# Combining three attention branches in the layout of the widest dilation instead of the plain order

## The chip, the cores and the metric

The kernel runs on one core of one Trainium2 chip. The metric is the device time of one execution in microseconds; less is better. A core has five engines that run side by side, each with its own ordered list of instructions: TensorE (PE in the profile; PEld is its loading of weights), VectorE (DVE), ScalarE (ACT), GpSimd (POOL) and SyncE (SP). SP computes nothing here; it issues nearly all DMA transfers, in order, and waits in that order for what each transfer needs. "SPq" marks its rows.

## The reference, cut to what matters

One decoder layer: a gated short convolution beside an attention mixer, then an output projection and a SwiGLU feed-forward part. The change touches only the attention. Each of 8 heads evaluates three branches, a window of 128 keys at distances of 1, 4 and 16 positions, and the three results are combined per position:

```python
DILATED_BRANCHES = ((128, 1), (512, 4), (2048, 16))      # window, dilation
SEQ, N_HEADS, HEAD_DIM = 2048, 8, 64

def dilated_mixture(q, k, v):
    outs, lses = [], []
    for window, dil in DILATED_BRANCHES:
        o, lse = dilated_branch(q, k, v, window, dil)    # query t sees keys t, t-dil, ..., t-window
        outs.append(o)
        lses.append(lse)
    w = jax.nn.softmax(jnp.stack(lses, axis=0), axis=0)
    o = jnp.sum(w[..., None] * jnp.stack(outs, axis=0).astype(jnp.float32), axis=0)
    return o.astype(q.dtype)
```

## The kernel before

The work goes in stages: input projection and convolution (to about 280 us of the profiled span), attention (about 280 to 805 us), output projection, and the feed-forward part (from about 970 us to the end). A scheduler fixes the order of each engine's instructions when the kernel is built, from the order in which the code asks for them and its own estimate of durations; the chip then keeps to that order.

In the attention stage the heads go in pairs: `g` is 0 to 3, `h` is 0 or 1, so heads are numbered 0 to 7 here as 2g + h. `attn_steps(g)` is a generator that computes the three branches `b` of the two heads: b = 0 is dilation 1, b = 1 dilation 4, b = 2 dilation 16. While it runs, `attention_pairs` interleaves the projections of the next pair (`qkv_steps`; tiles `mm`, matmuls of 128x384 from lines 187 to 189), or, beside the last heads, the rest of the convolution and the first output projections. So PE has two kinds of work in the stage, and what attention can't feed at once the projection fills.

A branch has 16 blocks of 128 queries. For b = 1 and b = 0 most steps take two blocks with two key blocks each; b = 1 has 7 steps, b = 0 has 8, and b = 2, where a block sees one key block, has 4 steps of four blocks. A step is a chain over all engines: PE makes the scores (`s`, lines 604 and 605), DVE adds the mask and takes the row's minimum (line 610, `accum_out` into column 65 of `u`), ACT takes the exponential (line 615), ACT and DVE split it into two halves (`eh`, lines 625 and 626), a DMA transposes them (`et<-eh`, issued by SP from line 195), and PE multiplies by the values (`av`, line 633). Steps of four blocks transpose on PE instead (`pt`, line 620; DVE then writes `et` at line 622). ACT copies `av` into the branch's result tile `u` (line 636), which holds 128 partitions x 16 blocks x 66 columns (64 outputs, the denominator, the minimum) in 32 bits, 528 KB in all.

The blocks of a branch lie in the branch's own layout. In b = 0, block n and partition p hold position 128n + p. In b = 2, block n and partition p hold position 16p + n. Before, the results are combined in the layout of b = 0: the branches run in the order 1, 2, 0; the results of b = 1 and b = 2 are stored to DRAM (`d_u<-u`, lines 642 and 645) and read back in the layout of b = 0 (`r<-d_u`, line 647), and `combine` runs when b = 0 is done. In `combine` DVE takes the minimum of the three columns 65 (lines 540 and 541), then three differences (543), ACT an exponential, POOL weights and adds the results (548 to 550, 554), and SP stores 64 columns for this head to `d_y` (557). For the last head DVE does POOL's part, four blocks at a time, and the result stays on chip (`y7`).

The tiles `r1` and `r2` have one buffer each, `u` has three, `v` (the branch's values, loaded from `d_v` by lines 518, 521 and 525) two, `mm` three.

Of the kernel before, what the change touches and what calls it, by code (L numbers as in the profile page):

```python
# [8 lines left out]
F32 = mybir.dt.float32  # L9
# [8 lines left out]
P = 128  # L18
# [3 lines left out]
NT = S // P  # L22
# [3 lines left out]
HD = 64  # L26
# [3 lines left out]
class Builder:  # L30
# [55 lines left out]
    def vmax(self, *xs):  # L86
# [4 lines left out]
        for i, x in enumerate(xs):  # L91
            e.tensor_reduce(a[:, i:i + 1], x, axis=AX.X, op=ALU.max, apply_absolute_value=True)
        if len(xs) == 2:
# [4 lines left out]
        q = self.wsm.tile([P, 1], F32, name="vm_q")  # L98
        e.tensor_reduce(q, t, axis=AX.X, op=ALU.max)
        r = self.wsm.tile([P, 1], F32, name="vm_r")  # L100
# [167 lines left out]
    def conv_steps(self, j, W, before=None, scratch=None):  # L268
# [12 lines left out]
        for c in range(S // NC):  # L281
# [25 lines left out]
            else:  # L307
# [11 lines left out]
            nc.sync.dma_start(self.d_ya[:, j, t], y)  # L319
            nc.vector.tensor_reduce(self.yamax[:, j * 4 + c:j * 4 + c + 1], y, axis=AX.X, op=ALU.max,  # L320
                                    apply_absolute_value=True)
# [119 lines left out]
    def qkv_steps(self, g, st):  # L441
# [12 lines left out]
        for i in range(0, NT, 4):  # L454
# [21 lines left out]
            ss = self.at.tile([P, 16], F32, name="qk_ss")  # L476
            nc.vector.tensor_reduce(ss, n, axis=AX.X, op=ALU.add)
            nc.vector.tensor_scalar(ss, ss, 1.0 / HD, EPS, op0=ALU.mult, op1=ALU.add)
# [28 lines left out]
    def attn_steps(self, g, st):  # L507

        nc = self.nc
        uv = self.at.tile([P, 1], F32, name="uv")  # L510
        nc.vector.tensor_scalar_mul(uv, st["u"], 2.0 ** 20)
        V, U, R = {}, {}, {}

        def load_v(h, b):
# [7 lines left out]
            else:  # L522

                for r in range(4):
                    nc.sync.dma_start(t[32 * r:32 * r + 32], dv.rearrange("(n p r) c -> r p n c", n=NT, r=4)[r])
        for h, b in [(h, b) for h in range(2) for b in (1, 2, 0)]:
            qT = st["qT"][h]
            ka, kl = (st[x][:, :, h] for x in ("ka", "kl"))
            load_v(h, b)
# [2 lines left out]
            last = g == 3 and h == 1  # L532

            def combine(c, n):

                ts = slice(c, c + n)
                bm = self.at.tile([P, NT], F32, name="bm", bufs=2)[:, 0:n]
                w = self.at.tile([P, 3, NT], F32, name="cw", bufs=2)[:, :, 0:n]
                X = [r[:, ts] for r in (U[h, 0], R[h, 1], R[h, 2])]
                nc.vector.tensor_tensor(bm, X[0][:, :, HD + 1], X[1][:, :, HD + 1], op=ALU.min)  # L540
                nc.vector.tensor_tensor(bm, bm, X[2][:, :, HD + 1], op=ALU.min)
                for q in range(3):
                    nc.vector.tensor_tensor(w[:, q], bm, X[q][:, :, HD + 1], op=ALU.subtract)
                nc.scalar.activation(w, w, AF.Exp)
                X = [x[:, :, 0:HD + 1] for x in X]
                e = nc.vector if last else nc.gpsimd
                for q in range(3):
                    e.tensor_tensor(X[q], X[q], w[:, q].unsqueeze(2).broadcast_to([P, n, HD + 1]), op=ALU.mult)
                e.tensor_tensor(X[1], X[1], X[2], op=ALU.add)
                e.tensor_tensor(X[0], X[0], X[1], op=ALU.add)  # L550
                nc.vector.reciprocal(bm, X[0][:, :, HD])
                nc.vector.tensor_scalar_mul(bm, bm, uv)
                y = self.y7[:, ts] if last else X[0][:, :, 0:HD]
                e.tensor_tensor(y, X[0][:, :, 0:HD], bm.unsqueeze(2).broadcast_to([P, n, HD]), op=ALU.mult)
                if not last:
                    i = (2 * g + h) * HD
                    nc.sync.dma_start(self.d_y.rearrange("(t p) c -> p t c", p=P)[:, :, i:i + HD], y)
            Ub = U[h, b] = self.up.tile([P, NT, HD + 2], F32, name="u", bufs=3)
            Vb = V[h, b]

# [26 lines left out]
            for u0 in (0, 8, 4, 12) if last and b == 0 else range(0, NT, 4):  # L587
# [48 lines left out]
                nc.scalar.copy(Ub[:, u0:u0 + 4, 0:HD + 1], av)  # L636
                if last and b == 0:
                    combine(u0, 4)
            if b > 0:
                du = self.d_u[2 * g + h][b - 1]  # L640
                if b == 1:
                    nc.sync.dma_start(du.rearrange("(n p r) c -> p n (r c)", n=4, r=4),
                                      Ub.rearrange("p (n r) c -> p n (r c)", n=4))
                else:
                    nc.sync.dma_start(du.rearrange("(p r) c -> p (r c)", r=16), Ub.rearrange("p r c -> p (r c)"))
                t = R[h, b] = self.up.tile([P, NT, HD + 2], F32, name=f"r{b}")
                nc.sync.dma_start(t, du.rearrange("(b p) c -> p b c", p=P))
            elif not last:
                combine(0, NT)

# [547 lines left out]
```

## Time and profile before

| what | value |
|---|---|
| median of 3 runs | 2199.84 us (2195.81 to 2200.91) |
| the profiled execution's own time | 2202.29 us |
| its span in the profile | 2200.5 us |
| mean granted TensorE clock | 0.981 |
| PE busy | 2070.1 us (94%) |
| DVE / ACT / POOL busy | 1454.9 / 1027.3 / 629.6 us |
| DMA packets | 555492, of them 354624 under 512 B |

The profiled execution lies 2.45 us above the median, within what the three runs scatter. Times inside the profile count from the start of the span. A matmul's row gives its whole passage through the array, so rows of consecutive matmuls overlap; how often PE can start one is read from the distance of their starts.

### The profile page before, as it was taken

To read this page: it belongs to the slowest core of one execution; us is meant where nothing else is said; L and a number is where in the kernel's file an instruction comes from. 1 tells how busy PE (TensorE), PEld (TensorE's weight loads), DVE (VectorE), ACT (ScalarE), POOL (GpSimd) and SP (SyncE) were. 2 spreads that over 40 slices of the span, in tenths; PEclk is the share of its full clock that TensorE was granted. 3 is DMA by queue.
4 is the path that set the end of the run, shared out by engine and by line. 5 is a ranking of instruction groups with operands and counts; after the bars stand their busy time and mean duration, and the time that the engine had idled before them with its cause. 6 is when DMAs were issued, how large, how long until landed. Compare 5 with 4: busy or idle time off the path is not lost. (4 is left out here: it accounts for less than half of the span.)

```text
span 2200.5 us, 32856 instructions
## 1 busy us (share of the span) xinstructions
PE 2070.1 (94%) x11864; PEld 1076.9 (49%) x11864; DVE 1454.9 (66%) x3380; ACT 1027.3 (47%) x2134; POOL 629.6 (29%) x515
## 2 busy tenths in 40 slices
PE   4899999989989879989899999999999999999999
PEld 2344567767666534433344444444444444444444
DVE  5687447778876677874776676766676565555554
ACT  6443347677776656661443343334333344344341
POOL 0000133244343212230321122212222235555463
PEclk9999999999999989999899999999999999999999
DMA  9777358999989989789322332233223554251342
GB/s 244 168 211 241 104 125 149 190 178 192 185 157 223 205 191 299 231 245 254 105 96 91 104 113 88 95 102 107 90 95 104 192 188 151 60 190 53 116 143 96
DMA packets 555492, 339.64 MB, mean 154 GB/s; under 512 B 354624, under 2 KB 508224, under 8 KB 552896
## 3 DMA queue, kind: packets, MB, share of 16 engines
q1 hardware_dynamic: 550320, 337.45, 58.8%
q8 instruction: 93, 1.52, 0.3%
q10 hardware_dynamic: 5008, 0.08, 0.1%
q14 instruction: 71, 0.58, 0.1%
HBM read 161.24 MB, written 107.54 MB: 122 GB/s over the span
## 5 line engine op out<-in xcount | busy, mean ns | idle before, releaser
L1002 PEld LDWEIGHTS <-w 128*128 128x128 f16 x3696 | 363.3, 98 | 472.1 <-issue 27.5
L1002 PE MATMUL ps<-b,w 128*128 128x512 f16 x2112 | 466.8, 382 | 16.8 <-DMA b<-d_h 7.1
L1120 PE MATMUL ps<-b,w 128*128 128x512 f16 x1848 | 399.3, 379 | 0.9 <-DVE s L1138 0.8
L1002 PE MATMUL ps<-hb,w 128*128 128x512 f16 x1584 | 351.2, 382 | 10.4 <-DVE s L1008 9.3
L1120 PEld LDWEIGHTS <-w 128*128 128x128 f16 x1848 | 180.8, 98 | 219.2 <-issue 1.4
L895 POOL TENSOR_TENSOR t<-wq 128x512 f32<-128x512 f32 (+1 forms) x46 | 59.2, 1286 | 440.5 <-issue 207.7
L187 PE MATMUL mm<-wq,b 128*128 128x384 f16 x512 | 170.6, 333 | 6.7 <-DVE vs L471 6.7
L1008 DVE TENSOR_TENSOR s<-ps,s 128x512 f32<-128x512 f32 x220 | 150.1, 683 | 39.8 <-PE ps L1002 39.1
L188 PE MATMUL mm<-wq,b 128*128 128x384 f16 x512 | 170.4, 333 | 0.0
L189 PE MATMUL mm<-wq,b 128*128 128x384 f16 x512 | 170.3, 333 | 0.0
L1127 POOL TENSOR_TENSOR x<-x,s 128x512 f32<-128x512 f32 x72 | 103.9, 1444 | 185.0 <-DVE s L1138 130.5
L1128 DVE SCALAR_TENSOR_TENSOR x<-ps,a_u,x 128x512 f32<-128x512 f32 x96 | 71.9, 749 | 112.7 <-PE ps L1120 82.8
L615 ACT ACTIVATE s<-s,u 128x256 f32<-128x256 f32 (+1 forms) x224 | 97.9, 452 | 68.3 <-DVE u L610 47.4
L610 DVE CUSTOM_DVE_ANT_0 s<-s,mask,nkap 128x256 f32<-128x256 f32 (+1 forms) x224 | 104.3, 482 | 19.2 <-PE s L605 13.4
L187 PEld LDWEIGHTS <-b 128*128 128x128 f16 x768 | 84.2, 110 | 65.0 <-DMA b<-b 7.5
L188 PEld LDWEIGHTS <-b 128*128 128x128 f16 x768 | 84.3, 110 | 62.9 <-issue 13.9
L189 PEld LDWEIGHTS <-b 128*128 128x128 f16 x768 | 84.1, 109 | 56.8 <-issue 5.1
L633 PE MATMUL av<-v,et 128*128 128x65 f16 x1800 | 77.8, 195 | 31.3 <-DMA et<-eh 20.3
L187 PE MATMUL cvx<-b,wq 128*128 128x512 f16 (+1 forms) x200 | 76.9, 388 | 31.8 <-ACT kb L262 25.0
L912 ACT CAST w<-t 128x512 f16<-128x512 f32 x88 | 53.6, 615 | 108.6 <-PE ps L1002 86.9
L604 PE MATMUL s<-ka,qT 128*128 128x128 f16 (+1 forms) x408 | 91.3, 270 | 8.6 <-DVE eh L626 7.6
L1107 ACT CAST w<-t 128x512 f16<-128x512 f32 (+1 forms) x96 | 53.7, 580 | 92.2 <-PE ps L1120 75.1
(297 smaller groups left out, 3792.0 us busy)
## 6 DMA issues: line engine op xcount, KB each, us to landing
d_a<-a SPq DMA_DIRECT2D x88, 256.0 KB, 2.0
d_wd<-w SPq DMA_DIRECT2D x77, 256.0 KB, 2.1
wq<-d_a SPq DMA_DIRECT2D x64, 256.0 KB, 4.3
b<-d_wd SPq DMA_DIRECT2D x14, 1024.0 KB, 6.0
wraw<-in_w_in_dram SPq DMA_DIRECT2D x24, 512.0 KB, 6.8
d_h<-hl SPq DMA_DIRECT2D x24, 512.0 KB, 3.7
wq<-in_w_gate_dram SPq DMA_DIRECT2D x22, 512.0 KB, 5.3
wq<-in_w_up_dram SPq DMA_DIRECT2D x22, 512.0 KB, 5.4
```

Source lines behind the costliest of these rows:

```text
L187: self.pe = mm(ps, lhsT=lh(k), rhs=rh(k), start=k == ks[0], stop=False)
L188: mm(ps, lhsT=lh(k), rhs=rl(k), start=False, stop=False)
L189: mm(ps, lhsT=ll(k), rhs=rh(k), start=False, stop=k == ks[-1])
L604: nc.tensor.matmul(o, lhsT=query(u), rhs=hi[x], start=True, stop=False)
L610: nc.vector.tensor_tensor_reduce(sm[:, at[u]], sp[:, at[u]], mask[:, P - P * has_prev(u):256], accum_out=Ub[:, u, HD + 1:HD + 2], op0=ALU.add,
L615: nc.scalar.activation(sm[:, at[u]], sm[:, at[u]], AF.Exp, scale=-1.0, bias=Ub[:, u, HD + 1:HD + 2])
L633: self.pe_av = nc.tensor.matmul(av[:, u - u0], lhsT=p_, rhs=v_, start=n_ == 0, stop=n_ == len(ops) - 1)
L1002: nc.tensor.matmul(ps[self.BANK[n]], lhsT=w[:, x, k], rhs=b[:, y, k], start=first and k == 0 and q == 0, stop=k == 3 and q == 2, skip_grou ...
L1008: nc.vector.tensor_tensor(t, x, y, op=ALU.add)
L1120: nc.tensor.matmul(ps[self.BANK[n]], lhsT=L[n][:, x, f], rhs=B[n][:, f, y], start=first and f == 0 and q == 0, stop=f == n_f - 1 and q == ...
L1127: nc.gpsimd.tensor_tensor(o, o, s_, op=ALU.add)
L1128: nc.vector.scalar_tensor_tensor(o, bank, u, o, op0=ALU.mult, op1=ALU.add)
```

## The change

For all heads but the last (g = 3, h = 1) the branches run in the order 1, 0, 2, and the combination is made in the layout of b = 2. The result of b = 2 now stays in its tile `u`. The results of b = 1 and b = 0 pass through DRAM: b = 1 is stored as before, b = 0 is stored in 2048 pieces of 264 B, and both are read back with 16 consecutive rows, 4224 B, for each partition. The store of the head's output to `d_y` addresses rows in the new layout; it is as many pieces of 256 B as before. The last head is computed as before. Bytes are the same everywhere; numbers of instructions on the computing engines are too.

```diff
-        for h, b in [(h, b) for h in range(2) for b in (1, 2, 0)]:
+        for h, b in [(h, b) for h in range(2) for b in ((1, 2, 0) if g == 3 and h == 1 else (1, 0, 2))]:
...
-                X = [r[:, ts] for r in (U[h, 0], R[h, 1], R[h, 2])]
+                X = [r[:, ts] for r in ((U[h, 0], R[h, 1], R[h, 2]) if last else (U[h, 2], R[h, 1], R[h, 0]))]
...
-                    nc.sync.dma_start(self.d_y.rearrange("(t p) c -> p t c", p=P)[:, :, i:i + HD], y)
+                    nc.sync.dma_start(self.d_y.rearrange("(p r) c -> p r c", r=NT)[:, :, i:i + HD], y)
...
-            if b > 0:
-                du = self.d_u[2 * g + h][b - 1]
+            if b != (0 if last else 2):
+                du = self.d_u[2 * g + h][b == 1]
                 if b == 1:
                     nc.sync.dma_start(du.rearrange("(n p r) c -> p n (r c)", n=4, r=4),
                                       Ub.rearrange("p (n r) c -> p n (r c)", n=4))
+                elif b == 0:
+                    nc.sync.dma_start(du.rearrange("(t p) c -> p t c", p=P), Ub)
                 else:
                     nc.sync.dma_start(du.rearrange("(p r) c -> p (r c)", r=16), Ub.rearrange("p r c -> p (r c)"))
-                t = R[h, b] = self.up.tile([P, NT, HD + 2], F32, name=f"r{b}")
-                nc.sync.dma_start(t, du.rearrange("(b p) c -> p b c", p=P))
+                t = R[h, b] = self.up.tile([P, NT, HD + 2], F32, name=f"r{1 if b == 1 else 2}")
+                if last:
+                    nc.sync.dma_start(t, du.rearrange("(b p) c -> p b c", p=P))
+                else:
+                    nc.sync.dma_start(t.rearrange("p r c -> p (r c)"), du.rearrange("(p r) c -> p (r c)", r=16))
```

After the change the lines behind 526 have moved by one (610 is 611, 541 is 542, 633 is 634, 626 is 627), and those of the round trip by more: 645 is 648 for the last head and 646 for the new store of b = 0, 647 is 651 for the last head and 653 for the others.

The order of the instructions shifts over the whole attention stage. Two places. The first is DVE's list at the end of head 4, around the second minimum of `combine`, which waits for the second result to come back from DRAM (`r_6992` before, `r_7096` after; `vs` is the split of the next pair's values out of PE's `mm`, `qT` a copy of its queries).

```order
L610 ISA sm,u<-s,mask,nkap 128x128
L610 ISA u 128x1
L610 ISA s,u<-s,mask,nkap 128x256
L610 ISA u 128x1
L610 ISA s,u<-s,mask,nkap 128x256
L610 ISA u 128x1
L541 TENSOR_TENSOR bm<-bm,r_6992 128x16
L543 TENSOR_TENSOR cw<-bm,u 128x16
```

```order
L541 TENSOR_TENSOR bm<-u,r_6744 128x16
L611 ISA s,u<-s,mask,nkap 128x256
L611 ISA u 128x1
L623 TENSOR_TENSOR et<-pt,et 128x512
L502 COPY qT<-qp 128x512 x2
L471 SCALAR_TENSOR_TENSOR vs_2123<-mm,vs_2123 128x2x64 x2
L611 ISA s,u<-s,mask,nkap 128x256
L611 ISA u 128x1
L542 TENSOR_TENSOR bm<-bm,r_7096 128x16
```

Before, the minimum stood behind the four masks of head 5's first step and the two of its second; after, it stands behind the second step's two and one of the third's, with a write of `et`, two copies of `qT` and two splits of `vs` ahead of it, and the first step's four masks come behind it. The branch whose return it waits for was, before, followed on PE by the 8 steps of b = 0, and is now followed by the 4 steps of b = 2.

The second place is SP's list around the second round trip of head 0 (`d_u_1_66` and `r_3336` before, `d_u_0_65` and `r_3500` after).

```order
L195 DMA_TRANSPOSE et<-eh 128x8x128
L645 DMA d_u_1_66<-u 128x1056
L518 DMA v<-d_v_61 128x4x520
L647 DMA r_3336<-d_u_1_66 128x16x66
L195 DMA_TRANSPOSE et<-eh 128x8x128 x3
```

```order
L195 DMA_TRANSPOSE kb<-qkhl 128x8x128
L646 DMA d_u_0_65<-u 128x16x66
L653 DMA r_3500<-d_u_0_65 128x1056
L473 DMA d_v_62<-vs_2123 128x2x520
L525 DMA v<-d_v_61 32x16x130
L195 DMA_TRANSPOSE et<-eh 128x8x128 x3
```

Before, a transpose of b = 0 stood ahead of the store and three more behind the load; after, the round trip stands in the four steps of b = 2, which need no DMA transposes, its load directly behind its store, and the four loads of b = 0's values for the next head (line 525) begin behind it.

## The prediction

> **What bounds the kernel now.** I read the split of the span by stages first, since the page's 94% for PE is a mean over stages.
>
> ```profile
> 0.00:320.00 320.00, 277.47 (x1404) 147.84 (x1405) 205.51 (x517) 142.72 (x291) 37.62 (x57) 0.98 0.70 181
> 320.00:805.00 485.00, 436.72 (x4244) 318.60 (x4243) 361.67 (x1313) 319.61 (x848) 162.90 (x124) 0.96 0.94 186
> 805.00:1103.00 298.00, 268.96 (x1189) 118.52 (x1188) 208.68 (x394) 155.17 (x278) 62.78 (x49) 0.94 0.82 224
> 1103.00:2200.50 1097.50, 1086.92 (x5030) 491.94 (x5028) 679.08 (x1157) 409.77 (x721) 366.26 (x285) 1.00 0.35 114
> ```
>
> The columns are the stretch, its length, busy time of PE, PE's weight loads, DVE, ACT and POOL, then the granted clock, the share of the 16 DMA engines and GB/s. The change lies in the second row. There PE is busy 436.7 of 485.0 us, so at most 48.3 us of idle time, and what the clock loses, can be won. The chain of work that ended last begins at about 1103 us and doesn't reach this stage, so I go by what PE waited for in it, line by line, with total, times and longest in us:
>
> ```profile
> PE av L633 <- DMA et<-eh: 20.3, 19, 3.2
> PE s L604 <- DVE eh L626: 7.6, 5, 4.2
> PE mm L187 <- DVE vs L471: 6.5, 5, 1.9
> PE av L633 <- DMA v<-d_v: 4.9, 1, 4.9
> PE av L633 <- ACT u L636: 4.2, 3, 1.8
> ```
>
> These name the last link, not the cause. The cause of the worst of them shows in the order of time around the end of heads 3 and 4 (start, length, engine, line; in brackets the idle time ahead and what ended it):
>
> ```profile
> 554.18 0.19 DVE L541 TENSOR_TENSOR bm<-bm,r 128x16 f32<-128x16 f32 x1 [4.45 <-DMA r<-d_u]
> ...
> 551.83 0.84 PE L633 MATMUL av<-v,et 128*128 128x65 f16 x12 [2.23 <-DMA et<-eh]
> 554.62 0.48 PE L187 MATMUL mm<-wq,b 128*128 128x384 f16 x1 [1.95 <-DVE vs L471]
> 554.90 0.52 PE L188 MATMUL mm<-wq,b 128*128 128x384 f16 x1
> 555.22 0.52 PE L189 MATMUL mm<-wq,b 128*128 128x384 f16 x1
> ...
> 611.54 0.19 DVE L541 TENSOR_TENSOR bm<-bm,r 128x16 f32<-128x16 f32 x1 [3.45 <-DMA r<-d_u]
> ...
> 612.97 0.32 PE L187 MATMUL mm<-wq,b 128*128 128x384 f16 x1 [1.54 <-DVE vs L471]
> 620.53 0.37 PE L604 MATMUL s<-ka,qT 128*128 128x256 f16 x1 [4.23 <-DVE eh L626]
> ```
>
> DVE stands for 4.45 us at the second minimum of the combination, because the branch result has not come back from DRAM. Everything DVE does for PE is queued behind it: the splits `vs` that free `mm`, the halves `eh`. PE loses 2.23 + 1.95 us there and 1.54 + 4.23 us at the next head. It also comes back slow: at 554.90 and 555.22 the starts are 0.32 us apart, and the stretch's clock was half.
>
> ```profile
> 550.50:554.00 3.50, 0.84 (x12) 0.74 (x13) 0.00 (x0) 2.52 (x8) 0.00 (x0) 0.68 1.34 240
> 554.00:558.00 4.00, 3.38 (x11) 1.58 (x11) 3.45 (x9) 2.06 (x5) 2.79 (x2) 0.50 1.22 160
> ```
>
> So such a wait costs about 2 us more behind it (4 us at 0.50). In the whole stage DVE waited like this 15.1 us (the row stands below).
>
> **The change part by part.** *The round trip through DRAM.* Its links are the store of the second branch, the load of it, and for the new kernel the nearest rows: the output store, whose 2048 pieces of 256 B are like the new store's 2048 of 264 B, and the load of b = 2's values, which like the new load takes one long piece per partition (4160 B against 4224 B). First the old store (645), the old load (647), then the output store (557) and the values' load (521):
>
> ```profile
> L645 SPq DMA_DIRECT2D d_u<-u x8: 345/532/1397, 364.1 to 769.6; - x8
> DMA to landing us min/median/max: 3.1/4.5/5.3
> ...
> L647 SPq DMA_DIRECT2D r<-d_u x16: 364/422/3672, 352.1 to 774.4; - x16
>   DVE bm L541: 15.1, 8
> DMA to landing us min/median/max: 4.4/5.9/8.0
> ...
> L557 SPq DMA_DIRECT2D d_y<-u x7: 360/434/572, 394.6 to 751.9; - x7
> DMA to landing us min/median/max: 4.1/4.3/6.2
> ...
> L521 SPq DMA_DIRECT2D v<-d_v x8: 342/552/769, 319.7 to 739.6; - x8
> DMA to landing us min/median/max: 3.9/4.8/5.9
> ```
>
> Before: 4.5 + 5.9 us, and about 1.6 us by my estimate for ACT's copy of the last `av` and SP's queue, 12.0 us in all. After: 4.3 + 4.8 + 1.6 = 10.7 us. From both sides: 4.1 + 3.9 + 1.6 = 9.6 and 6.2 + 5.9 + 1.6 = 13.7 us.
>
> Against it stands the time that PE can go on. I counted along PE's rows in both orders from the last `av` of the branch that is sent away to the first PE row that needs something behind DVE's second minimum. The starts in this piece of the trace give the steps of the count:
>
> ```profile
> 544.84 0.33 PE L187 MATMUL mm<-wq,b 128*128 128x384 f16 x1
> 545.00 0.33 PE L188 MATMUL mm<-wq,b 128*128 128x384 f16 x1
> ...
> 545.97 0.27 PE L604 MATMUL s<-ka,qT 128*128 128x256 f16 x1
> 546.08 0.27 PE L605 MATMUL s<-kb,qT 128*128 128x256 f16 x1
> ...
> 546.41 0.98 PE L633 MATMUL av<-v,et 128*128 128x65 f16 x24
> 547.23 0.41 PE L620 MATMUL pt<-ident,sm 128*128 128x128 f32 x2
> 547.48 0.27 PE L604 MATMUL s<-ka,qT 128*128 128x256 f16 x1
> ...
> et<-eh SPq DMA_TRANSPOSE x110, 4.3
> ```
>
> That is 0.16 us for a 384-wide matmul, 0.11 for a 256-wide one, 0.82/24 = 0.034 for an `av`, 0.25/2 = 0.12 for a `pt`; where the need is an `eh`, 5.5 us go off for the transpose (4.3 in the last row, 1.2 by estimate for the split and SP's issue). The allowances for heads 0 to 6 come to 10.5, 7.7, 8.8, 10.4, 9.4, 14.1 and 13.4 us before, and 13.0, 7.4, 12.4, 11.3, 7.1, 15.0 and 8.2 us after. Their means are 10.6 and 10.6: four steps of b = 2 give no less room than eight of b = 0, since the scheduler put as much projection into them. With 12.0 us, PE is short by 1.5 + 4.3 + 3.2 + 1.6 + 2.6 = 13.2 us before; that is the size of the four waits quoted (9.95 us for heads 3 and 4) with some for the rest. With 10.7 us, it is short by 3.3 + 3.6 + 2.5 = 9.4 us after, in heads 1, 4 and 6. This term is 9.4 - 13.2 = -3.8 us. Its ends are 6.1 - 13.2 = -7.1 us at 9.6 us, and 0.7 + 6.3 + 1.3 + 2.4 + 6.6 + 5.5 - 13.2 = +9.6 us at 13.7 us.
>
> *The half clock behind waits.* Two waits of over 3 us before (heads 3 and 4) cost about 2 us each; after, heads 1 and 4 come out at 3.3 and 3.6 us. I take -0.5 us, between -4 (none left) and +4 us (four).
>
> *The packets.* Per head, a load of 2048 pieces becomes one of 128 twice, and a store of 128 one of 2048: 1920 fewer, 13,440 for seven heads.
>
> ```profile
> DMA packets 242383, 90.35 MB, mean 186 GB/s; under 512 B 220816, under 2 KB 238486, under 8 KB 242070
> ...
> q1 hardware_dynamic: 242326, 89.61, 93.1%
> ```
>
> At the stage's mean of 0.931 x 485 x 16 / 242,326 = 0.030 us per packet, that is at most 13,440 x 0.030 / 16 = 25 us less on each engine; by bytes, which stay, it is nothing. Long pieces take longer each, so I go for 10 us of 451, 2%. PE feels it only in its 20.3 us of waits for `et`: 2% to 5% of the transposes' 4.3 us, 0.1 to 0.2 us at 19 waits, up to -4 us. I take -1.0 us. The transfers also move: b = 0's values and the head's output now load the b = 1 steps, which need transposes, and b = 2's steps are relieved, which do not; so +2 us is the other end.
>
> *The end of the stage.* Behind the last `av` PE has, of the 96 matmuls of the first output projections, 31 left before and 39 after, while the last combination runs its chain to `y7` and on to the transposes. PE then waits for those:
>
> ```profile
> 812.38 0.61 PE L187 MATMUL mm<-b,b 128*128 128x512 f16 x1 [7.04 <-DMA b<-b]
> ```
>
> Eight more 512-wide matmuls at 0.16 x 512 / 384 = 0.22 us fill 1.7 of the 7.04 us, and the last `av` comes as much earlier. I take -1.7 us; 0 is the other end, if the last branch is late for its own reasons.
>
> *What costs nothing.* The output store has the same pieces; its landing hides behind the next head. POOL's share is the same, with 162.9 of 485 us busy. The first minimum (541 after) needs b = 1, back long before. SP waits for the store's landing ahead of the load, as before; queued behind it is now mostly traffic for later steps, no transposes of b = 2, so nothing on PE's path; if that cover is gone it costs up to the store's 4.3 us in a head. Order on PE from the middle of the output projections on is unchanged.
>
> **Sum.** -3.8 - 0.5 - 1.0 - 1.7 = -7.0 us. Against the profiled execution's own 2202.3 us that gives 2195.3; its offset to the median is 2.4 us, so for the median 2199.8 - 7.0 = 2192.8 us.
>
> **A rule that speaks against it.** The old store of b = 2 lands in 4.5 us and the output store with small pieces in 4.3 us, so small pieces cost no more here. The Trainium skill, "DMA: Bandwidth & Descriptors", section "Specifications", says that transfers under 512 B go below line rate because the DMA engine reads, modifies and writes; by that rule the new store would be the slower one. The rows disagree with it for this size of store, as far as landing shows it; what it would do is the first rival.
>
> **The rivals.** *Slower: the return of b = 0 comes late.* Between its last `av` and the end of the head stand 4 steps where there were 8. If the new store lands late, all allowances are missed. Price by round trip: at 13.7 us +9.6 us in the first term, +4 us of half clock, with the other two terms as they are +10.9, so 2210.7 us. It decides from about 12.5 us on, where the short times (0 + 5.1 + 0.1 + 1.2 + 5.4 + 4.3 = 16.1 us) eat what the other terms bring. For it: three allowances of 7 to 8 us. Against it: the landing rows above, and that store and load now follow each other directly. *No change: the waits only move.* PE's 20.3 us for `et` come back in b = 0, whose work now starts behind b = 1 with less projection between scores and `av` in heads 0 to 2, 14.5 us on the mean where it was 16.4 by the same count; with the first term at +0.8 us (12.0 us again, 14.0 us short), -0.5 us of half clock, and the gains of packets and tail lost in it, the time is about 2200.1 us. For it: DMA engines at 0.94, which leave no slack for a reordering.
>
> **How the numbers follow.** Forecast 0.46, no change 0.29, slower 0.25. This measurement can tell about 0.2%, 4.4 us, from no change. Of the forecast's case a little ends within that; I give faster 0.46, same 0.28, slower 0.26. The range reaches from -7.1 - 4 - 4 - 1.7 = -16.8 us, 2183 us, to the slower rival's 2210 us; the forecast's own range is 2185 to 2196 us.
>
> **What would show it.** Right: DVE's wait for `r` at the second minimum falls from 15.1 to about 10 us; the new store (646) lands in about 4.3 us, the new loads (653) in about 4.8; the wait at about 812 us falls to about 5.3 us; PE's idle time in the stage falls from 48 to about 42 us. Wrong: DVE waits over 4 us in heads 1, 4 and 6 with PE's `vs` and `eh` waits behind; or `et` waits of 20 us or more, now in b = 0.

## The result, and the profile after

The changed kernel takes 2238.74 us (median of four runs, 2237.22 to 2239.9), the kernel before 2200.38 us beside it: a ratio of 1.0177, 95% interval 1.016 to 1.0195, or 38 us slower. The forecast was 2192.8 us with 2183 to 2210 as range. It was wrong in sign, and the time lies outside the range.

The split by stages again, same columns as in the prediction. The last stage, 1097.5 us before, is cut off at its old length, so that the first row here (the kernel before) and the second (the changed kernel) cover the same work, from 320 us to the end of the output projection, to within a few us. The two rows behind them are of line 187 in the output projection, first before, then after (count, shortest, median and longest in ns, first and last start in us).

```profile
320.00:1103.00 783.00, 705.68 (x5431) 437.12 (x5431) 570.34 (x1707) 474.78 (x1125) 225.68 (x173) 0.96 0.89 201
```

```profile
320.00:1140.60 820.60, 713.78 (x5423) 440.86 (x5423) 560.35 (x1706) 477.80 (x1127) 224.15 (x173) 0.94 0.85 191
```

```profile
L187 PE MATMUL ps<-b,b x112: 379/379/634, 817.5 to 960.5; 128*128 128x512 f16 x112
```

```profile
L187 PE MATMUL ps<-b,b x112: 379/379/379, 855.5 to 997.9; 128*128 128x512 f16 x112
```

The stretch is 37.6 us longer, as the span is. These matmuls begin 38.0 us later and end 37.4 us later, so the loss is complete when the output projection begins; the projections of the first pair of heads begin at 239.9 us before and 241.1 after. All but about 1 us of the loss therefore lies in attention. Of the 37.6 us, PE's rows with work grew by 8.1 us (705.68 to 713.78, clock 0.96 to 0.94, with the same number of matmuls but for missing records). The rest is idle time: all of PE's waits in the stretch add up to 78.3 us before and 106.7 us after, +28.4 (the list of waits misses about 1 us of the rest).

What PE waited for in the changed kernel, total, times and longest in us:

```profile
PE s L605 <- DVE eh L627: 29.3, 14, 6.2
PE av L634 <- DMA et<-eh: 17.5, 16, 4.8
PE mm L187 <- DVE vs L471: 9.2, 5, 3.3
...
PE mm L187 <- ACT b L779: 5.0, 1, 5.0
```

The waits for transposes fell a little (20.3 before). The waits for the score buffers, which DVE's half `eh` frees, rose from 7.6 to 29.3. The new store (646), the new loads (653), and what DVE and SP waited for because of them:

```profile
L646 SPq DMA_DIRECT2D d_u<-u x7: 359/458/1368, 374.4 to 767.2; - x7
DMA to landing us min/median/max: 7.8/8.7/9.7
...
L653 SPq DMA_DIRECT2D r<-d_u x14: 332/342/720, 352.3 to 775.4; - x14
DMA to landing us min/median/max: 3.3/4.2/6.8
...
DVE bm L542 <- DMA r<-d_u: 21.2, 6, 7.8
...
SPq L653 <- DMA d_u<-u: 38.1, 8, 8.0
SPq L525 <- PE av L634: 24.0, 4, 7.2
```

The store lands in 8.7 us where I had put 4.3. SP stands 38.1 us for it (8.1 before), and 24.0 us at the value loads of b = 0 for the last `av` of b = 2 (4.6 us for an `av` before). The two rows of the kernel before:

```profile
SPq L647 <- DMA d_u<-u: 8.1, 6, 2.6
...
SPq L525 <- PE av L633: 4.6, 2, 4.1
```

One place shows what that does, the end of head 1, in order of time: SP, DVE, PE, and the clock of the wait and of the 2.8 us behind it.

```profile
443.22 0.38 SPq L518 DMA_DIRECT2D v<-d_v  x1
444.28 0.36 SPq L646 DMA_DIRECT2D d_u<-u  x1
452.75 0.33 SPq L653 DMA_DIRECT2D r<-d_u  x1
453.20 0.36 SPq L473 DMA_DIRECT2D d_v<-vs  x1
453.67 16.27 SPq L195 DMA_TRANSPOSE et<-eh  x4
...
457.16 0.19 DVE L542 TENSOR_TENSOR bm<-bm,r 128x16 f32<-128x16 f32 x1 [3.00 <-DMA r<-d_u]
...
462.23 0.37 PE L605 MATMUL s<-ka,qT 128*128 128x256 f16 x1 [6.16 <-DVE eh L627]
...
456.00:462.20 6.20, 0.07 (x3) 0.00 (x0) 4.90 (x19) 4.32 (x12) 2.58 (x2) 0.69 0.76 89
462.20:465.00 2.80, 1.89 (x8) 1.26 (x8) 2.80 (x5) 0.41 (x1) 1.23 (x1) 0.50 0.49 94
```

The store goes out at 444.28; the load behind it only at 452.75, and the four transposes of the next head's first steps behind both. DVE stands 3.00 us at the second minimum; masks, the combination's differences and the next pair's norms are queued behind it, and the `eh` that PE needs starts at about 461.5. PE stands 6.16 us and goes on at a clock of 0.50. It is the mechanism of the prediction's "slower" rival, at a larger size than that rival was given.

The chain of work that ended last says the same of the whole stage. In the kernel before it could be followed back to about 1103 us only; here it runs through attention, and through all seven of the new stores, 61.4 us in sum, with six of their loads behind them (start and length in us):

```profile
374.45 7.78 DMA d_u<-u
...
444.28 8.40 DMA d_u<-u
...
505.39 8.69 DMA d_u<-u
...
572.72 9.31 DMA d_u<-u
...
632.42 9.70 DMA d_u<-u
...
697.10 9.35 DMA d_u<-u
...
767.20 8.15 DMA d_u<-u
```

### The profile page after: what moved, and what is told of

It is laid out like the page before. It is cut to its first block, busy times and chain, and to the rows that moved or that the text cites. A ratio compares the mean times of both kernels' runs of the same rounds, so it can differ in the third digit from the quotient of the medians.

```text
span 2238.1 us, 32856 instructions
## 1 busy us (share of the span) xinstructions
PE 2079.5 (93%) x11864; PEld 1081.3 (48%) x11864; DVE 1446.4 (65%) x3380; ACT 1030.5 (46%) x2134; POOL 626.5 (28%) x515
## 2 busy tenths in 40 slices
DMA packets 542052, 339.64 MB, mean 152 GB/s; under 512 B 340288, under 2 KB 493888, under 8 KB 539456
## 4 chain that ended last, share of the span: by engine, by line
PE 56%; DMA 16%; DVE 13%; ACT 5%; issue 4%; SPq 4%; POOL 1%; DVEq 0%; ACTq 0%; POOLq 0%
PE ps L1008 25%; PE ps L1126 18%; DMA d_u<-u 3%; PE mm L187 3%; PE mm L188 3%; PE mm L189 2%; DMA et<-eh 2%; SPq L195 2%; DMA wq<-in_w_up_dram 2%; PE av L634 1%; DMA qp<-qkhl 1%; DMA wraw<-in_w_in_dram 1%; DMA r<-d_u 1%; DMA wq<-in_w_gate_dram 1%; DVE s L611 1%
## 5 line engine op out<-in xcount | busy, mean ns | idle before, releaser
L1008 PE MATMUL ps<-b,w 128*128 128x512 f16 x2112 | 466.5, 381 | 16.6 <-DMA b<-d_h 7.2
L605 PE MATMUL s<-ka,qT 128*128 128x128 f16 (+1 forms) x408 | 94.1, 275 | 30.2 <-DVE eh L627 29.3
L634 PE MATMUL av<-v,et 128*128 128x65 f16 x1800 | 80.2, 197 | 31.3 <-DMA et<-eh 17.5
L634 PEld LDWEIGHTS <-et 128*128 128x128 f16 x1800 | 73.5, 100 | 54.6 <-DMA et<-eh 22.2
```

The costliest lines, as they stand in the source:

```text
L605: nc.tensor.matmul(o, lhsT=query(u), rhs=hi[x], start=True, stop=False)
L634: self.pe_av = nc.tensor.matmul(av[:, u - u0], lhsT=p_, rhs=v_, start=n_ == 0, stop=n_ == len(ops) - 1)
L1008: nc.tensor.matmul(ps[self.BANK[n]], lhsT=w[:, x, k], rhs=b[:, y, k], start=first and k == 0 and q == 0, stop=k == 3 and q == 2, skip_grou ...
```

## The experiments

"Leaves out" in a text on record tells which part of the computation a kernel doesn't do. The letters of theories are those of these texts. They speak of lines of 64 B: that size is an assumption of mine, which the sizes tried fit; no run measures it.

**1. What a store of small pieces costs by itself.** A kernel of nothing but transfers, one at a time, five times round, 128 partitions x 16 pieces:

```diff
+nc.sync.dma_start(a264.rearrange(tp, p=P), u)                                # 264 B, packed
+nc.sync.dma_start(b264.rearrange(tp, p=P)[:, :, 0:64], u[:, :, 0:64])        # 256 B at 264 B steps
+nc.sync.dma_start(c256.rearrange(tp, p=P), u[:, :, 0:64])                    # 256 B, packed
...
+nc.sync.dma_start(e320.rearrange(tp, p=P)[:, :, 0:66], u)                    # 264 B at 320 B steps
+nc.sync.dma_start(f320.rearrange(tp, p=P), w)                                # 320 B, packed
...
+nc.sync.dma_start(h264.rearrange("(p r) c -> p (r c)", r=NT), u.rearrange("p r c -> p (r c)"))
```

> This kernel does none of the layer: it only stores and reloads a tile through DRAM, one transfer at a time, five times each, so that each landing time stands alone. Stores: (33) 264 B pieces packed at 264 B, as the changed kernel stores b = 0; (35) 256 B pieces at steps of 264 B; (37) 256 B pieces packed; (39) 256 B pieces at steps of 2048 B, as the output store; (41) 264 B pieces at steps of 320 B; (43) 320 B pieces packed; (45) 264 B pieces at steps of 512 B; (47) 4224 B for each partition, as before; (49) 512 B pieces packed. Theory A, pieces that begin or end inside a 64 B line are what is slow: 33 and 35 about 7 us, 41 and 45 about 6 to 7, and 37, 39, 43, 49 under 4.5, 47 about 3. Theory B, any piece under 512 B is slow by itself: 33, 35, 37, 39, 41, 43, 45 alike, about 7 us, and 49 and 47 fast. Theory C, the store is slow only beside the other traffic of the attention stage: all but 49 (twice the bytes) at 4.5 us or less.

The view of transfers, with KB each and the median time to landing in us: `a` 264 B packed and the load of it, `b` 256 B at steps of 264, `c` 256 B packed, `d` 256 B at steps of 2048, `e` 264 B at steps of 320, `f` 320 B packed, `h` 4224 B for each partition.

```profile
a<-big SPq DMA_DIRECT2D x5, 528.0 KB, 6.8
big<-a SPq DMA_DIRECT2D x5, 528.0 KB, 4.2
...
b<-big SPq DMA_DIRECT2D x5, 512.0 KB, 6.6
c<-big SPq DMA_DIRECT2D x5, 512.0 KB, 3.8
d<-big SPq DMA_DIRECT2D x5, 512.0 KB, 4.1
...
e<-big SPq DMA_DIRECT2D x5, 528.0 KB, 5.2
f<-big SPq DMA_DIRECT2D x5, 640.0 KB, 4.2
...
h<-big SPq DMA_DIRECT2D x5, 528.0 KB, 2.6
```

The number and size of pieces are not what makes this store slow: 256 B pieces land in 3.8 us packed and in 6.6 us at steps of 264 B, with the same bytes. Most of the cost is in where a piece begins and ends. Some is in the count or size: 128 long pieces take 2.6 us. With starts at multiples of 320 B the 264 B pieces take 5.2, and 320 B pieces that leave no gap 4.2 although they are longer. Reading the packed 264 B rows back costs nothing of the kind (4.2 us). Theory A was right on the order of these rows, but not on every size: 264 B pieces at steps of 320 and 512 B landed in 5.2 and 5.0 us, under its 6 to 7, and 512 B pieces, with twice the bytes, in 5.1, over its 4.5. Theories B and C fall.

The Trainium skill, "DMA: Bandwidth & Descriptors", section "Specifications", puts the loss on transfers under 512 B, by read, modify and write. The direction was right here and I dismissed it; a size under 512 B is not what tells these rows apart, since 256 B and 320 B packed land faster than 264 B packed. That short pieces lose something as well is not excluded by them.

**2. The changed kernel with the long store.**

```diff
-    nc.sync.dma_start(du.rearrange("(t p) c -> p t c", p=P), Ub)
+    nc.sync.dma_start(du.rearrange("(p r) c -> p (r c)", r=16), Ub.rearrange("p r c -> p (r c)"))
```

> The changed kernel with the store of b = 0 made as 4224 B for each partition, which leaves out the change of layout of b = 0 (its rows come back in other places); all else is the same. Theory 1, the slow landing of the store with 264 B pieces (8.7 us against 4.5) is the cause: the store lands in about 4.5 us, SP waits for it about 10 us in all where it waited 38, and the time is 2192 to 2206 us. Theory 2, the place is the cause, four steps of b = 2 are too few for the round trip and the new order is worse in itself: 2225 us or more.

2217.9 us, ratio 1.0089 [1.0063, 1.0114]: 20.8 us of the loss go with the store, 18 us stay. The time lies between the two theories' ranges. (Its profiled execution was the fastest of four, 2212.36 us, 5.5 us under the median.) Its waits of DVE's second minimum, SP and PE:

```profile
DVE bm L542 <- DMA r<-d_u: 4.6, 4, 1.5
...
SPq L653 <- DMA d_u<-u: 10.6, 3, 5.4
SPq L525 <- PE av L634: 16.5, 3, 7.1
...
PE av L634 <- DMA et<-eh: 19.9, 18, 3.8
PE s L605 <- DVE eh L627: 16.4, 12, 3.7
```

The text says that all else is the same. The work is, the built order is not: a changed store shifts the scheduler's order here and in all the edits below. At the end of head 1 the load of b = 1's values now stands behind the store, where it stood ahead of it in the changed kernel:

```profile
438.77 0.53 SPq L646 DMA_DIRECT2D d_u<-u  x1
439.39 0.39 SPq L518 DMA_DIRECT2D v<-d_v  x1
```

So the 20.8 us are the store's landing (4.2 us) together with the order that came with it.

**3. The kernel before with small pieces.** Here b = 2's store is made of 264 B pieces in the old order of branches.

```diff
-    nc.sync.dma_start(du.rearrange("(p r) c -> p (r c)", r=16), Ub.rearrange("p r c -> p (r c)"))
+    nc.sync.dma_start(du.rearrange("(t p) c -> p t c", p=P), Ub)
```

> The kernel before with the store of b = 2 made in 264 B pieces for all heads but the last, which leaves out its right layout (its rows come back in other places); branch order, loads and combination as before. Theory 1: the store lands in 8 to 9 us here too, and the time rises by 20 to 35 us, to 2220 to 2235 us. Theory 2, the place matters: eight steps of b = 0 cover a slow store, and the time stays under 2210 us.

2214.76 us, 1.0075 [1.0051, 1.0099]: +15 us with the form of the store as the only edit (the built order shifts with it), under theory 1's 20 to 35 and over theory 2's 2210 us. It lands in 8.3 us (7.8 to 9.2), as in the changed kernel, and DVE's wait at the second minimum goes from 15.1 to 22.1 us. So the store is slow in either order of branches.

**4. The load of b = 0 issued by GpSimd,** so that SP doesn't stand for the store.

```diff
-    nc.sync.dma_start(t.rearrange("p r c -> p (r c)"), du.rearrange(...))
+    q = nc.gpsimd if b == 0 else nc.sync
+    q.dma_start(t.rearrange("p r c -> p (r c)"), du.rearrange(...))
```

> The changed kernel with the load of b = 0's result issued by GpSimd instead of SyncE, so that GpSimd and not SP stands waiting for the store; the store stays slow. Theory 1a, what costs is SP standing in front of the load (38 us), with the transposes queued behind: the wait for the queries' transposes at line 502 falls from 32 to about 15 us and the time to 2205 to 2215 us. Theory 1b, what costs is DVE standing at the second minimum for a late result (21 us): the time stays at 2228 us or more.

2248.55 us, 1.023 [1.0205, 1.0256], 10 us worse. The store still lands in 8.5 us; GpSimd stood 44.3 us for it in four waits of up to 14.7 us, and the load went out later, so that DVE's wait grew from 21.2 to 31.2 us. It doesn't clear SP, since a later load came with it; the wait at line 502 fell from 32.2 to 26.3 us, not to 15. That a longer wait of DVE costs time agrees with it.

**5. Order 0, 1, 2,** which puts b = 1 and b = 2 between b = 0's store and the combination.

```diff
-    ((1, 2, 0) if g == 3 and h == 1 else (1, 0, 2))
+    ((1, 2, 0) if g == 3 and h == 1 else (0, 1, 2))
```

> The changed kernel with the branches of all heads but the last in the order 0, 1, 2. The slow store of b = 0 then has 11 steps behind it instead of 4, and the result that comes back last is b = 1's, whose store in pieces of 1056 B landed in 4.8 us. Theory 1b, DVE standing for a late result is what the slow store costs: the wait at the second minimum falls from 21 to under 8 us and the time to 2208 to 2222 us. Theory 1a, SP standing in front of the load is what costs, and that stays: 2230 us or more.

2233.5 us, 1.017 [1.0139, 1.0201]. DVE waits 15.4 us at its minimum, as in the kernel before, SP 11.4 us for the store; still 35 us are lost. Neither text had this: SP's wait did not stay, and DVE's did not fall under 8. So neither the late return of a result at the minimum nor SP's wait for the store is the whole of it.

**6. and 7. The combination three steps later,** in the changed kernel and in the kernel before, so that DVE reaches the minimum when the results are long there.

```diff
-    combine(0, NT)
+    self.waiting = combine
...
+    if self.waiting and b == 1 and us[0] == (0, 4, 6, 8, 10)[2]:
+        with self.tc.issue_after(sub.ins):
+            self.waiting(0, NT)
+        self.waiting = None
```

> The changed kernel with the combination of a head asked for three steps later, behind DVE's part of the second step of two blocks of the next head's b = 1, so that DVE reaches the second minimum later; transfers are unchanged. Theory 1b, DVE's standing (21 us) is a large part: the wait falls under 8 us and the time to 2218 to 2230 us. Theory 1a, SP's standing (38 us): 2233 to 2243 us.

> The kernel before with the same later combination. If DVE's 15 us of standing at the second minimum cost PE time, as the prediction had it: the wait falls under 5 us and the time by 4 to 12 us, to 2188 to 2196 us. If other work fills PE there, or POOL's later part of the combination costs as much: 2196 to 2206 us.

The changed kernel gains 8 us (2230.72, 1.0163 [1.0138, 1.0187]) with DVE's wait down from 21.2 to 5.4 us, just short of theory 1b's 2230. The kernel before loses 10 us (2208.15, 1.0054 [1.0038, 1.0069]) although DVE's wait of 15.1 us is gone; PE's waits in the stretch rose from 78.3 to 87 us. DVE stood elsewhere instead: its wait for the transposes of the next pair's queries (line 502) rose from 16.6 to 27.2 us. So this edit, which shifts the built order too, did not win the 15 us of DVE's waiting, which the prediction's first term had taken as there to be won.

**8. Does a mere shift of order cost?** The kernel before, projection steps bound one attention step nearer.

```diff
-    rate, lag = (4.52, 3.49, 3.2, 2.1)[g], (12, 12, 13, 8)[g]
+    rate, lag = (4.52, 3.49, 3.2, 2.1)[g], (11, 11, 12, 8)[g]
```

> The kernel before with the projection of the next pair queued behind attention steps that are one step nearer (11, 11, 12 for 12, 12, 13 steps back), which only shifts the order. It shows what a shift of the order by itself does. Theory 3a, what is left with the fast store (18 us) is more than a shift of the order costs: this kernel is within 8 us of the kernel before, 2191 to 2207 us. Theory 3b, any shift of this order costs that much: 2212 us or more.

2197.83 us, 1.0002 [0.9988, 1.0016]: nothing, as theory 3a has it. It is one shift of one kernel; experiments 12 and 17 show shifts that cost 12 and 11 us.

**9. Pieces that begin at multiples of 320 B, in place.** All of the computation kept.

```diff
-    dr.tile([S, HD + 2], F32, ...)
+    dr.tile([S, HD + 2 if b or h == H - 1 else 80], F32, ...)
...
+    nc.sync.dma_start(du[:, 0:HD + 2].rearrange("(t p) c -> p t c", p=P), Ub)
...
+    nc.sync.dma_start(t, du[:, 0:HD + 2].rearrange("(p r) c -> p r c", r=16))
```

> The changed kernel, but the rows of b = 0's results lie 320 B apart in DRAM (80 words instead of 66), so that each 264 B piece begins at a multiple of 64 B and shares no 64 B line with another. Nothing else is changed but b = 0's load, which becomes 2048 pieces of 264 B. Theory A (pieces that share lines are slow): alone such a store landed in 5.2 instead of 6.8 us, so here line 646 lands in about 6.5 to 7 instead of 8.7 us, SP's wait for it falls from 38 to about 25 us, and the time falls from 2238 to about 2226 to 2232. Rival B (pieces under 512 B are slow, wherever they begin): landing 8.7 us as before, and at 2238 or more, since the load has 1920 pieces more.

2221.98 us, 1.0117 [1.0093, 1.0142]: 16.8 us faster than the changed kernel, with the steps of the rows as the only edit (the built order shifts here too), and although the load now takes 2048 pieces. Landing and SP's wait:

```profile
DMA to landing us min/median/max: 5.6/7.4/8.1
...
SPq L653 <- DMA d_u<-u: 28.1, 6, 7.2
```

The time lies at the better end of what theory A gave, the landing a little over its 6.5 to 7. Rival B (8.7 us, no gain) falls.

**10. to 12. What stays with the fast store.** SP stands ahead of the value loads with transposes behind it. In the first run these loads are asked for later; in the others only the interleaving is shifted. All three have the long store of experiment 2.

```diff
+    x = self.behind.get(b)                    # b = 0: a transpose of b = 1's third wide step
+    with self.tc.issue_after(x.ins) if x is not None else nullcontext():
+        load_v_(h, b)                         # b = 1: the store of b = 0
```

> The changed kernel with the long store of b = 0 (4224 B for each partition; leaves out the change of layout of b = 0) as in e1_long_store, and the value loads moved later in SP's list: those of b = 0 behind the transposes of the third wide step of b = 1, those of b = 1 between the store and the load of b = 0's results. Same transfers. Theory D (the 18 us that stay with the fast store come from SP standing ahead of the value loads, 21.6 us at line 525 and 23.7 us at line 518, before transposes): these waits fall to about 5 us each, PE's waits for the score buffer (s <- eh) from 16.4 to about 8, the time from 2218 to about 2203 to 2208. Theory E (the new order of instructions fits worse in many places, none of them a queue's): 2212 to 2222. If the loads land too late, av waits for v rise over 4.5 us and the time over 2222.

> The changed kernel with the long store of b = 0 (leaves out the change of layout of b = 0), and the projection steps bound to attention steps that lie 11, 11, 12 instead of 12, 12, 13 back. The same edit of the kernel before moved it by 0.0%. Theory E (the interleaving, set for the order 1, 2, 0, fits the order 1, 0, 2 badly): a change of it moves the time by 5 us or more, up or down. Theory D: within 4 us of e1_long_store's 2218.

> As e1_lag11, with the projection steps bound to attention steps 14, 14, 15, 9 back, so they may come earlier on PE's list. Theory E: moves by 5 us or more, up or down, and if the order is what fits badly, one of this and e1_lag11 lies below 2212. Theory D: within 4 us of 2218.

With later value loads 2206.45 us, 1.004 [1.0026, 1.0053]: 11.5 us faster than the long store alone. The waits (line numbers are moved: 530 was 525, 523 was 518):

```profile
SPq L523 <- DMA d_v<-vs: 6.5, 1, 6.5
...
SPq L530 <- PE av L641: 6.0, 2, 5.8
...
PE s L610 <- DVE eh L632: 24.2, 15, 7.9
PE av L641 <- DMA et<-eh: 11.1, 13, 2.3
```

SP's waits fell as expected. PE's gain is not where I had put it: its waits for the score buffer rose, those for transposes fell from 19.9 to 11.1 us, and the sum of all fell from 85.7 to 80.4. The two shifts of the interleaving gave 2212.46 (1.0073 [1.0048, 1.0097]) and 2230.23 us (1.0152 [1.0119, 1.0185]): -5 and +12 us. The first edit had moved the kernel before by nothing. Theory D holds by the time, not by the waits it named. That the interleaving matters with the new order of branches, as theory E has it, holds too, though neither shift came below its 2212 us.

**13. to 16. With the computation kept.** Pieces of 320 B that leave no gap (each takes 14 words of the next row along), the later value loads, both, and both with the shifted interleaving.

```diff
+    x = t[:, 0:NT * (HD + 2)].rearrange("p (r c) -> p r c", c=HD + 2)
+    a = [list(q) for q in x.ap]
+    a[-1][1] = 80
+    return bass.AP(tensor=x.tensor, offset=x.offset, ap=a)
```

> As a_pitch320, but each piece is 320 B long and fills its five lines of 64 B (it takes 14 words of the next row along, which nobody reads). 21% more bytes in this store, no line written in part. Alone, 320 B pieces landed in 4.2 us, 264 B pieces at the same steps in 5.2. Theory A (lines written in part are what costs): line 646 lands in 5.5 to 6.5 instead of 7.4 us, SP's wait for it falls from 28 to about 20 us, and the time from 2222 to 2214 to 2219. Rival F (in the crowded stage the count of pieces is what costs): 7.4 us or more, 2220 to 2226.

> The changed kernel with its slow store, and only the value loads moved later in SP's list as in e1_values_later. If the two causes add, the time falls by the same 11 us, from 2238 to 2225 to 2230. If SP's place is taken by its wait for the slow store, the move brings less than 5 us: 2233 to 2240.

> Whole lines and later value loads together, all of the computation kept. If both causes hold and add: 2217 - 11 = 2203 to 2209. If they cover each other: 2212 to 2218.

> As a_lines_and_values, with the projection steps bound 11, 11, 12 attention steps back, which was worth 5 us with the long store. If the interleaving's fit is the rest of the loss, 2198 to 2204, as the kernel before; if that gain was the same waits for SP, no change against a_lines_and_values.

| kernel | us | ratio | store's landing, us |
|---|---|---|---|
| 320 B pieces | 2224.9 | 1.0126 [1.0111, 1.0142] | 6.8 |
| later value loads alone | 2240.44 | 1.0203 [1.0184, 1.0221] | 7.9 |
| both | 2212.68 | 1.0076 [1.0057, 1.0094] | 4.7 |
| both, interleaving shifted | 2214.81 | 1.0081 [1.0057, 1.0105] | 4.7 |

The landing of "later value loads alone", and what SP stood for there:

```profile
DMA to landing us min/median/max: 7.5/7.9/8.5
...
SPq L653 <- ACT u L644: 27.1, 5, 6.8
SPq L660 <- DMA d_u<-u: 20.6, 4, 6.2
```

Filling the gaps gained nothing over experiment 9 in time, though the store landed 0.6 us sooner: theory A missed, and the time is as rival F had it. In that kernel GpSimd stood 51.1 us for the store before it could write the fill words, which may hide a gain. Later value loads bring 12 us where the store is fast (2224.9 to 2212.68, as 2217.9 to 2206.45) and nothing where it is slow: there SP stands at the store and the load instead, so the two causes cover each other, as the second half of that text had it. The edit has a second effect, which its texts don't name: the load of b = 1's values, 520 KB, stood directly ahead of the store in five of seven heads and now comes behind it, and the store lands in 4.7 instead of 6.8 us. The 12 us are the two together. "Both" came out 3.7 us over the expected 2203 to 2209, inside the 2212 to 2218 given for causes that cover each other; but its gain is the full 12 us, and what the text had too low is the time of the 320 B pieces, 2224.9 instead of 2217 us. The shifted interleaving gave nothing more (2 us over, intervals overlapping), so its 5 us in experiment 11 did not carry over.

**17. The fill words of the 320 B pieces written by DVE.** In 13 to 16 GpSimd writes the 14 words behind the last row of a tile; with both edits together it stood 46 us for it, by the profile.

```diff
-    nc.gpsimd.memset(Uf[:, NT * (HD + 2):], 0.0)
+    with self.tc.issue_after(self.sub.ins):
+        nc.vector.memset(Uf[:, NT * (HD + 2):], 0.0)
```

> As a_lines_and_values, but the 14 words behind the last row of each tile are filled by DVE behind a split in the last steps of b = 1, where the tile is long free, and not by GpSimd, which stood 46 us for it ahead of the combination's work. All of the computation is kept. If GpSimd's standing is what keeps this version 6 us over e1_values_later: 2204 to 2209, which would leave 5 to 10 us over the kernel before. If GpSimd's standing costs nothing: 2210 to 2215 again, and the rest is the piecewise store's landing (4.7 against 3.2 us) and its pieces on the DMA engines.

2223.6 us, 1.0117 [1.01, 1.0134]: 11 us worse, neither of the two expectations. The instruction itself takes 70 ns, seven times. The stretch from 320 us on, first for "both" and then for this kernel:

```profile
320.00:1114.10 794.10, 714.02 (x5422) 442.11 (x5422) 568.83 (x1703) 474.93 (x1120) 223.91 (x179) 0.94 0.87 199
```

```profile
320.00:1124.30 804.30, 711.70 (x5413) 440.42 (x5413) 567.79 (x1710) 476.87 (x1125) 223.02 (x173) 0.94 0.86 196
```

The work is the same, the idle time 12.5 us more (80.1 against 92.6 us, lengths less PE's busy time). The built order of the whole stage shifts with such an edit; which of the shifted rows costs is not settled.

## Why the prediction was wrong, point by point

- **The step that failed first: the price of the new store.** It was priced at 4.3 us by the output store, whose pieces have 256 B. It took 8.7. The 8 B more were not the difference in kind: the output's pieces begin at multiples of 256 B, the new ones at multiples of 264 B, and experiment 1 shows this alone to be worth 2.8 us (3.8 against 6.6) on idle queues. The upper end, 6.2 us, was the output store's slowest landing, which bounds nothing about other steps of the rows. No row of the trace of before had such a store. The long store gave 20.8 us back, the steps of 320 B 16.8, each with the shift of the built order that came with it.
- **By its own working,** with the round trip at 8.7 + 4.2 + 1.6 = 14.5 us, the first term becomes 1.5 + 7.1 + 2.1 + 3.2 + 7.4 + 6.3 - 13.2 = +14.4 us. PE's waits grew by 28.4. So half of it is a term that the working did not have.
- **"What costs nothing": SP's wait for the landing.** I wrote that no transposes on PE's path are queued behind it. The rows at 453.67 show four of them behind the load, those of the next head's first steps, whose scores PE makes beside b = 2's steps. SP stood 38.1 us at the load instead of 8.1, and 24.0 instead of 4.6 at the value loads of b = 0, which the prediction did not look at. Moving those loads gave 11.5 us with the fast store, part of it perhaps because that store then landed in 3.2 instead of 4.2 us. The cover that I named (b = 2 needs no transposes) was true of b = 2 alone. PE's own waits for `et` did not grow (20.3 and 17.5 us); what grew is DVE's wait for the transposes of the next pair's queries at line 502, 16.6 us before and 32.2 after. It was 26.0 with the long store and 16.6 again with the later value loads as well.
- **The half clock** was put at -0.5 us, +4 at most. PE's busy time grew by 8.1 us for the same matmuls, the granted clock fell from 0.96 to 0.94.
- **The base of the first term.** 13.2 us of the kernel before's idle time were put down to DVE's second minimum and priced as to be won. Taking that wait away in the kernel before (experiment 7) made it slower by 10 us, in an order that had shifted too. The wait was real; that PE pays for it one to one was not shown.
- **Right:** the new load (4.2 us, 4.8 expected), the 13,440 packets fewer (555,492 to 542,052), and the direction of the waits for transposes (20.3 to 17.5 us; -1.0 with ends at -4 and +2). At the end of the stage, the wait at about 812 us and the one before it (`b` from ACT) sum to 9.7 us before and 7.7 after, near the -1.7 expected. These gains were there, and small.
- **The rival** "the return of b = 0 comes late" was the right mechanism, with a chance of 0.25 and a price of +10.9 us at a round trip of 13.7 us. It lacked SP's queue and the clock.
- **What stays open.** No run separates a store's landing from the order that shifts with it. For the landing speaks that four comparisons go the same way: 20.8 and 16.8 us (experiments 2 and 9), 15 us in the old order (experiment 3), and 28 us between "later value loads alone" and "both", more than any shift without a change of the work gave. With the long store and later value loads 7 to 9 us remain (by the medians; ratio 1.0026 to 1.0053), 17 us with the computation kept. Edits that change no work moved kernels with the new order of branches by -5, +12 and +11 us (experiments 11, 12 and 17). I take the rest for the fit of the built order to the new order of branches, which is argued, not shown. No version tried beats the kernel before.

## What to carry to other kernels

Price a transfer by a row with the same steps in DRAM, not only the same size and count of pieces; rows of 264 B, one after another from many partitions, are a different store from rows of 256 B, and where the profile has no such row, a small kernel of bare transfers tells it. When a wait on a queue's issuer is called free, list what stands behind it in the queue up to the next thing that some engine needs, other branches and heads included. A wait that ends last before an engine's idle time is not yet a price: here an edit that removed it made the kernel slower. And look whether an edit to one transfer shifts the built order of the rest before a difference is put down to that transfer.

## What the runs showed of the hardware that was not expected

A store of 2048 pieces of 256 B landed in 3.8 us packed, 4.1 us at steps of 2048 B, and 6.6 us at steps of 264 B, each time alone on the chip's queues; loads of these layouts took 4.1 to 4.4 us. In the crowded stage the store of packed 264 B pieces took 8.7 us, that at steps of 320 B 7.4, without gaps 6.8, and 4.7 when the load of b = 1's values, which stood directly ahead of it on SP's list in five of seven heads, came behind it. The long store went from 4.2 to 3.2 us by the same move. In experiment 2's own trace the load of b = 1's values stands directly ahead of three of the seven long stores: these land in 5.1 to 5.9 us, the other four in 2.9 to 4.2. So what the long store takes to land there depends on what was put on the queue just ahead of it. For the pieces this is less clear: without that load directly ahead, two of the gapless 320 B stores of experiment 13 took 5.6 and 7.1 us, the five with it 6.5 to 7.1.
